# A hybrid decoder layer: the narrow projection groups chained in PSUM, and W_out's plain blocks split early and stored

## The chip, the core and the metric

The kernel runs on one core of one Trainium2 chip. The metric is the device time of one execution in microseconds (us). The engines go by the profile's names: PE multiplies matrices (PEld loads its weights), DVE works elementwise, ACT evaluates functions and copies, POOL is a second, slower elementwise engine, and SP only issues transfers. Transfers can be issued by SP, ACT and POOL; each of these works through its instructions in order, and an issue that waits holds up what is behind it on its queue.

## The reference

One layer over 2048 tokens of width 1024, in float32:

```
n = rmsnorm(x);  proj = n @ w_in          # 3088 columns: gq gk gv gr glow dq dk dv
o_a = gated linear attention(gq, gk, gv, gate from glow), normed, times silu(gr)
o_b = dilated sliding-window attention(dq, dk, dv), three (window, dilation) pairs, with a bias table
h = x + [o_a ; o_b] @ w_out
h = h + square(relu(rmsnorm(h) @ w_ff1)) @ w_ff2
y = rmsnorm(h)
```

## The kernel before

**Exact products from two parts.** Matmuls run in a reduced float type. So each operand is split into a high part (an ACT copy) and a low part (a DVE subtraction), and `mm3` (L139 to L142) adds three matmuls: high by high, low by high, high by low. The helper `split` (L489 to L491) does the two instructions for one tile.

**Products of blocks.** The big products use a seven-multiplication scheme on two-by-two blocks: the two halves of the tokens or of the columns, and the two halves of the inner dimension. Sums of blocks are formed in SBUF ahead, the products are numbered 1 to 7, and the result blocks c11, c12, c21 and c22 are sums of products.

**The stages.** First the projection (`jobs`, L749 to L768, about 20 to 520 us), then attention, with the gated linear attention woven into it (`units`, L1242 to L1266, to about 865 us), then the product with W_out (L1556 to L1610), then the two MLP products.

**The projection.** The tokens are taken in two halves. In each half there are nine groups of W_in's columns (`groups`, L249): `dv`, then `gr` with the gate's 16 columns (264 wide), then six narrow ones (`dq`, `dk`, `dq`, `dk`, `gq`, `gk`, 2 x 128 columns), then `gv`. A narrow group puts the weights on the stationary side and streams 512 tokens, so one of its products is 12 matmuls of 512 columns; a product of a wide group is 4 x 12 matmuls of 256 or 264. A job is one product of one group. Each job first prepares the weights of the job after next (`prep`, L278: an ACT copy and a DVE subtraction into one of three `wcomb` buffers, and sums of weight blocks in the two `wraw` buffers, with the next group's loads behind them, `load_w`, L267), then multiplies (`product`, L400) into a PSUM bank, and then `rest` (L422) reads the bank.

Before, every product has a bank of its own, taken in turn ("acao", L372). ACT copies products 1, 5 and 4 (L440, L445, L453); DVE adds for products 2, 6, 3 and 7 (L442, L447, L448, L450, L455) and makes two more sums (L458). `outputs` (L323) exchanges the buffers of c12 and c22 from group to group. `finish` (L329) stores a result block: for `dq` and `dk` it splits it first (L341, L342), for `gr` it works out a log-sigmoid, an exponential and two products (one on POOL, L355), and for the block with the gate's columns `gate` (L308 to L321) transposes, multiplies once on PE and works out another log-sigmoid. Every load of W_in and every store goes through SP. The last two sums of the last job are put off into the attention stage (`late`, L368, L462, L1188).

In the second half the token blocks of that half are made ready beside the products (`second_half`, `OTHER`), and the rows of the attention bias are worked out (`bias_rows`, L469) and spread in DRAM (`spread_bias`).

**W_out.** The rows of some token tiles are multiplied plainly ("plain blocks" of W_out, called 1, 12, 2 and 3: the two column halves of inner rows 0 to 511 and of inner rows 512 to 1023); the other tiles use the seven products, for which blocks 5, 6, 4 and 7 are sums that POOL makes in attention (`sum_wo`) and `mix_wo` splits. The plain blocks are loaded in the last 28 units of attention, 128 rows every third unit (`load_wo`, L1115, called at L1240), and split there: two times 128x512 for inner rows 0 to 511 (`wb`), 128x1024 for the others (`wo`).

**The first MLP product.** Blocks of W1 (256 columns) are loaded through POOL (`load_w1`, L1381), two transfers of 512 KB each; the first two are asked for at the end of the W_out stage (L1607), and `prep1` (L1389) splits them.

**What orders the work.** From L739 on the program's order is a priority, not a fixed order: the compiler plans the order of each engine's instructions with a model of their durations, and the engines then follow that order strictly. `keep_in_program_order` pins an instruction behind the one that the program gives its engine just before it. All big tiles of SBUF come from 25 slots of one size, handed out when the last reader of the old content is done; PSUM's eight banks have the tags a (2), c (3), d (2) and o (1).

## Time and profile before

| | |
|---|---|
| median of 3 runs | 2244.66 us (2239.35 to 2244.89) |
| the profiled execution | 2242.91 us |
| its span on the core | 2241.1 us |
| mean granted clock of PE | 0.997 |
| busy: PE, DVE, ACT, POOL | 99%, 75%, 56%, 24% |
| moved by DMA | 491.79 MB, mean 219 GB/s |

A matmul's record is longer than its turn: the next starts before its end, so the busy time of PE says where PE stood still, not how fast it went. How fast it went is read from the number of matmuls in a stretch and from the granted clock. A group of instructions has, after its count, its busy time and mean duration in ns, and behind the second bar the idle time of its engine just before it, with what ended it. In the view of waits the three numbers are the total in us, how often, and the longest.

### The profile page before, as it was taken

The numbers are of one execution on the slowest core, as the hardware profiler recorded it, in microseconds if no ns is written. First come the engines' busy times: TensorE is split into PE (matmuls) and PEld (weight loads), VectorE is DVE, ScalarE is ACT, GpSimd is POOL, SyncE is SP. The second block draws the span as 40 slices with busy tenths as digits, with TensorE's granted clock in tenths as the row PEclk, the third lists the DMA queues.
The fourth block names the chain that finished last, engine by engine and source line by source line (L and its number), as shares of the span: only waits on it lengthen the run. The fifth ranks groups of instructions, "written<-read, shape, count | busy, mean of one in ns | idle before, by whom it ended". The sixth has DMA issues, their size and how long they took to land.

```text
span 2241.1 us, 35330 instructions
## 1 busy us (share of the span) xinstructions
PE 2212.8 (99%) x12420; PEld 1918.8 (86%) x12420; DVE 1680.8 (75%) x3173; ACT 1253.5 (56%) x2506; POOL 533.6 (24%) x535
## 2 busy tenths in 40 slices
PE   9999999999999999999999999999999999999998
PEld 8978998799999998887888888888888888888877
DVE  8787868666677677778777788777685697576798
ACT  7675446435787785555655566555555433333446
POOL 1110001016577673000000000000006222031462
PEclk9999999999999999999999999999999999999999
DMA  6467854787977877767744456555489988677775
GB/s 214 141 188 229 256 165 121 213 250 251 312 256 222 271 214 241 247 225 249 220 141 149 140 177 199 165 167 167 130 279 287 306 282 276 216 250 253 250 258 197
DMA packets 340934, 491.79 MB, mean 219 GB/s; under 512 B 20503, under 2 KB 237162, under 8 KB 330004
## 3 DMA queue, kind: packets, MB, share of 16 engines
q1 hardware_dynamic: 319842, 394.88, 54.6%
q0 software_dynamic: 13568, 41.95, 7.6%
q10 hardware_dynamic: 7346, 52.70, 6.3%
q8 instruction: 98, 1.61, 0.3%
q14 instruction: 80, 0.66, 0.1%
HBM read 335.52 MB, written 158.66 MB: 221 GB/s over the span
## 4 chain that ended last, share of the span: by engine, by line
PE 68%; issue 16%; DVE 7%; DMA 5%; POOL 2%; ACT 1%; SPq 0%; POOLq 0%; ACTq 0%; DVEq 0%
PE ps_a L141 7%; PE ps_a L142 6%; PE ps_a L140 6%; PE ps_c L141 5%; PE ps_c L142 5%; PE ps_c L140 5%; PE ps_a L909 4%; PE ps_d L141 3%; PE ps_d L142 3%; PE ps_d L140 3%; PE ps_o L141 3%; PE ps_o L140 3%; PE ps_o L142 3%; PE ps_d L890 3%; PE ps_c L872 2%
## 5 line engine op out<-in xcount | busy, mean ns | idle before, releaser
L490 ACT ACTIVATE cb<-bs 128x1024 fp32r<-128x1024 f32 x104 | 110.1, 1059 | 287.9 <-PE ps_o L141 94.6
L491 DVE TENSOR_TENSOR cb<-bs,cb 128x1024 fp32r<-128x1024 f32 x104 | 157.9, 1519 | 137.7 <-ACT cb L490 137.4
L1680 POOL TENSOR_TENSOR bs<-bs,rb 128x1024 f32<-128x1024 f32 x60 | 174.3, 2912 | 318.1 <-DMA bs<-w_ff 282.4
L491 DVE TENSOR_TENSOR w1comb<-w1raw,w1comb 128x512 fp32r<-128x512 f32 x224 | 153.2, 686 | 94.0 <-ACT w1comb L490 93.9
L1387 POOL DMA_DIRECT2D w1raw<-w_ff x64 | 48.2, 754 | 702.6 <-DVE w1comb L491 532.8
L490 ACT ACTIVATE w1comb<-w1raw 128x512 fp32r<-128x512 f32 x224 | 139.9, 627 | 92.0 <-PE ps_c L142 27.2
L881 ACT ACTIVATE pe<-pe,O 128x256 f32<-128x256 f32 (+1 forms) x384 | 157.5, 454 | 45.6 <-DVE O L880 41.9
L909 PE MATMUL ps_a<-v,pt 128*128 128x65 f32 x1200 | 180.8, 253 | 1.5 <-DVE pt L899 1.4
L909 PEld LDWEIGHTS ps_a<-v,pt 128*128 128x128 f32 x1200 | 175.7, 195 | 2.9 <-DVE pt L899 1.7
L880 DVE CUSTOM_DVE_ANT_0 pe<-ps_c,nb 128x256 f32<-128x256 f32 (+1 forms) x384 | 126.7, 360 | 46.8 <-PE ps_d L890 16.5
L890 PE MATMUL ps_d<-ident,pe 128*128 128x128 f32 x600 | 160.5, 281 | 0.0
L288 ACT ACTIVATE wcomb<-wraw 128x512 fp32r<-128x512 f32 (+2 forms) x119 | 90.1, 757 | 99.2 <-PE ps_a L141 33.0
L140 PE MATMUL ps_c<-hb,w1comb 128*128 128x512 f32 x320 | 124.6, 390 | 0.0
L141 PE MATMUL ps_c<-hb,w1comb 128*128 128x512 f32 x320 | 124.4, 389 | 0.0
L142 PE MATMUL ps_c<-hb,w1comb 128*128 128x512 f32 x320 | 124.1, 389 | 0.0
L491 DVE TENSOR_TENSOR ca<-ra,ca 128x1024 fp32r<-128x1024 f32 x84 | 121.8, 1451 | 0.1
L141 PE MATMUL ps_c<-cb,ca 128*128 128x512 f32 x312 | 121.5, 389 | 0.0
L140 PE MATMUL ps_c<-cb,ca 128*128 128x512 f32 x312 | 121.5, 389 | 0.0
L142 PE MATMUL ps_c<-cb,ca 128*128 128x512 f32 x312 | 121.4, 389 | 0.0
L890 PEld LDWEIGHTS ps_d<-ident,pe 128*128 128x128 f32 x600 | 109.2, 186 | 0.3
L355 POOL TENSOR_TENSOR acc<-acc,misc 128x264 f32<-128x264 f32 (+1 forms) x32 | 29.4, 924 | 319.3 <-DVE acc L354 303.9
L140 PE MATMUL ps_a<-wcomb,tb 128*128 128x256 f32 (+1 forms) x344 | 97.7, 284 | 0.0
(476 smaller groups left out, 7248.8 us busy)
## 6 DMA issues: line engine op xcount, KB each, us to landing
ra<-actD ACTq DMA_DIRECT2D x50, 1024.0 KB, 7.3
actD<-ring SPq DMA_DIRECT2D x176, 256.0 KB, 3.1
rb<-w_ff SPq DMA_DIRECT2D x88, 512.0 KB, 5.3
bs<-w_ff SPq DMA_DIRECT2D x72, 512.0 KB, 6.0
w1raw<-w_ff POOLq DMA_DIRECT2D x64, 512.0 KB, 5.3
k<-kD SPq DMA_DIRECT2D x16, 1024.0 KB, 7.9
rb<-hTD SPq DMA_DIRECT2D x28, 512.0 KB, 5.8
wraw<-w_in SPq DMA_DIRECT2D x48, 256.0 KB, 3.6
```

What stands on the lines that cost most here:

```text
L140: T.matmul(out, sh, mh, start=first, stop=False, **kw)
L141: T.matmul(out, sl, mh, start=False, stop=False, **kw)
L142: T.matmul(out, sh, ml, start=False, stop=last, **kw)
L288: A.activation(hi, src, AF.Copy, scale=sc)
L490: A.activation(hi, src, AF.Copy)
L491: V.tensor_tensor(lo, src, hi.bitcast(F32), op=OP.subtract)
L880: V.tensor_tensor_reduce(p, s, bias, scale=1.0, scalar=BIG, op0=OP.add, op1=OP.min, accum_out=nm)
L881: A.activation(p, p, AF.Exp, bias=nm, scale=-1.0)
L890: T.transpose(pb[:, i * 128:i * 128 + 128], src, ident)
L909: T.matmul(self.b.opsum[:, n % 4], self.pt[:, i * 128:i * 128 + 128], self.b.v[:, blk, cols], start=first, stop=last)
L1387: G.dma_start(raw1[g % 2][:, 4 * k:4 * k + 4], w1[:, 4 * k:4 * k + 4, g0:g0 + 256])
L1680: (engines or ((G,), (V, V))[len(sums) - 1])[e].tensor_tensor(v, v, r, op=OP.add if op == "+" else OP.subtract)
```

## The change

1. **Narrow groups chained.** The order of products is 1, 2, 6, 5, 7, 3, 4 there. Products 6, 7 and 4 are added in PSUM to product 1's bank, and 3 to product 5's; between two links the bank is read. So ACT copies three banks (after 1, 6 and 5), DVE adds three times (2, 7, 3), and c21 is read straight from the bank. The order of the wide groups becomes 1, 2, 5, 6, 3, 7, 4.
2. **Loads.** Two narrow groups share the two `wraw` buffers by halves, so that the next narrow group is asked for while this one is worked on. Wide groups from the third on load through POOL, and `gr`'s stores go through POOL.
3. **Backlog of `gr`.** Its c21 block is finished by one token tile in each of the next four narrow jobs, and the gate's product on PE comes one product later than its transpose. The postponed sums of the last job are gone. `bias_rows` is cut in three steps, and its PSUM tag changes.
4. **W_out.** In the second half's narrow groups two to five, `split_wo` loads W_out through POOL (128 rows, 512 KB, at a time), splits it in 16 pieces of 128x512 (four to a group, two behind the job of product 6 and two behind that of product 5, in two piece buffers), and stores high and low parts through POOL (512 KB a piece). In attention eight transfers of 1 MB, one every third unit, take the place of load and split.
5. **W1.** The second block is loaded as four transfers, the first half of its columns first.

```diff
-    order = (1, 2, 5, 6, 3, 4, 7)
-    jobs = [(g, j) for g in range(2 * NG) for j in order]
+    order, linked = (1, 2, 5, 6, 3, 7, 4), (1, 2, 6, 5, 7, 3, 4)
+    chained = lambda g: groups[g % NG][2] == 128
+    jobs = [(g, j) for g in range(2 * NG) for j in (linked if chained(g) else order)]
+    swapped = [False, False]
+    for g in range(2, 2 * NG):
+        swapped.append(swapped[-1] == chained(g - 1))
...
+    def raw_of(g, n):
+
+        w = groups[g % NG][2]
+        if w > 128:
+            return raws[n][:, :, :, :w]
+        return view(raw_slots[n][:, GP * (g % NG % 2):], (2, 4, 128))
...
-            SP.dma_start(raws[n][:, k, :, :w], w_in[:, 4 * k:4 * k + 4, c0 + n * w:c0 + n * w + w])
+            (SP if g < 2 or chained(g) else G).dma_start(raw_of(g, n)[:, k], w_in[:, 4 * k:4 * k + 4, c0 + n * w:c0 + n * w + w])
...
+        if chained(g):
+            if j == 2:
+                V.tensor_tensor(a11, a21, a11, op=OP.subtract)
+                V.tensor_tensor(a12, a12, a11, op=OP.subtract)
+            if j == 6:
+                V.tensor_tensor(a11, a22, a11, op=OP.subtract)
...
+        for n, k in FREE[g][j]:
+            load_w(g + 1, n, k)
+
+    FREE = {}
+    for g in range(2 * NG):
+        if not chained(g):
+            FREE[g] = {5: [(0, 0)], 3: [(0, 1)], 4: [(1, 1)], 7: [(1, 0)]}
+            if chained(g + 1):
+                FREE[g] = {5: [(0, 0), (0, 1)], 7: [(1, 0), (1, 1)]}
+        elif chained(g + 1):
+            FREE[g] = {1: [(0, 0)], 2: [(0, 1)], 6: [(1, 1)], 5: [(1, 0)]}
+        else:
+            FREE[g] = {1: [(0, 0)], 2: [(1, 0)], 3: [(0, 1)], 4: [(1, 1)]}
...
-            SP.dma_start(srD[tk, j:j + m], s[:, :m])
+            G.dma_start(srD[tk, j:j + m], s[:, :m])
...
-        if e == 0:
-            held[j, i] = bank()
-        p = held[j, i - e]
+        root = {6: 1, 7: 1, 4: 1, 3: 5}.get(j, j) if chained(g) else j
+        if e == 0 and root == j:
+            held[j, i] = ps({1: "a", 2: "c", 5: "oc"[g % 2]}[j]) if chained(g) else bank()
+        p = held[root, i - e]
...
+            if chained(g):
+                if j in (1, 6):
+                    A.activation(ix, q, AF.Copy)
+                elif j == 5:
+                    A.activation(i22, q, AF.Copy)
+                elif j == 4 and kind in ("dq", "dk"):
+                    done((1, 0), q=q)
+                elif j == 4:
+                    A.activation(i21, q, AF.Copy)
+                    done((1, 0))
+                else:
+                    v, y, of = {2: (i11, ix, (0, 0)), 7: (i22, i22, (1, 1)), 3: (i12, ix, (0, 1))}[j]
+                    V.tensor_tensor(v, q, y, op=OP.add)
+                    done(of)
...
+                if kind == "gr":
+                    behind.append((done, (1, 0)))
+                else:
+                    done((1, 0))
...
+    def split_wo():
+
+        raw, pieces = view(slot("wsum"), (2, D)), view(slot("wsplit", FR), (2, 2, 512))
+        for c in range(2):
+            G.dma_start(raw[:, c], wo[:, c])
+        yield
+        for n in range(16):
+            c, h = divmod(n, 2)
+            p = pieces[:, h]
+            r = raw[:, c % 2, 512 * h:512 * h + 512]
+            tc.keep_in_program_order(A.activation(p[:, 0], r, AF.Copy))
+            V.tensor_tensor(p[:, 1], r, p[:, 0].bitcast(F32), op=OP.subtract)
+            G.dma_start(wsD[((1, 12), (2, 3))[c // 4][h]][c % 4 // 2, :, c % 2], p.bitcast(F32))
+            if h and c < 6:
+                G.dma_start(raw[:, c % 2], wo[:, c + 2])
+            yield
...
+        if at == 7 * NG + 9:
+            next(of_wo)
+        if NG + 3 <= g < NG + 7 and jobs[at][1] in (6, 5):
+            for _ in range(2):
+                next(of_wo)
...
-    def load_wo(n):
-        for _ in range(n):
-            c = (4, 0, 1, 5, 2, 3, 6, 7)[len(loaded)]
-            loaded.append(c)
-            raw = slot("woraw")[:, :D]
-            SP.dma_start(raw, wo[:, c])
-            if c < 4:
-                for j, n in ((1, 0), (12, 1)):
-                    split(*block_view(j, c), raw[:, 512 * n:512 * n + 512])
-            else:
-                w = WO[c - 4] = view(slot("wo", FR), (2, D))
-                split(w[:, 0], w[:, 1], raw)
+    def load_wo(j, h):
+
+        t = slot(f"wb{j}", FR, 2048)
+        WB[j, h] = view(t, (2, 2, 512))
+        SP.dma_start(t.bitcast(F32), wsD[j][h].rearrange("p c i n -> p (c i n)"))
...
-        at_unit(NU - 28 + 3 * i + AHEAD, load_wo, 1)
+        at_unit(NU - 28 + 3 * i + AHEAD, load_wo, *((1, 0), (12, 0), (1, 1), (12, 1), (2, 0), (3, 0), (2, 1), (3, 1))[i])
...
-            for k in halves:
-                G.dma_start(raw1[g % 2][:, 4 * k:4 * k + 4], w1[:, 4 * k:4 * k + 4, g0:g0 + 256])
+            for n in range(2) if g == 1 else (None,):
+                cs = slice(0, 256) if n is None else slice(128 * n, 128 * n + 128)
+                for k in halves:
+                    G.dma_start(raw1[g % 2][:, 4 * k:4 * k + 4, cs], w1[:, 4 * k:4 * k + 4, g0:g0 + 256][:, :, cs])
```

124 lines of the change are left out of this document (66 added, 58 removed).

## The prediction

> **What bounds the kernel now.** I read the busy shares first, then matmul counts and the granted clock by stage, then what TensorE waited for, and last the order of time around each wait.
>
> ```profile
> span 2241.1 us, 35330 instructions
> PE 2212.8 (99%) x12420; PEld 1918.8 (86%) x12420; DVE 1680.8 (75%) x3173; ACT 1253.5 (56%) x2506; POOL 533.6 (24%) x535
> ```
>
> TensorE is busy for 99% of the span and idle for 2241.1 - 2212.8 = 28.3 us. The change takes no matmul out, so all it can win is idle time, and time at a low clock. Busy time hides the second, so the stages come next (columns: the stretch and its length, then busy time and count of PE, PEld, DVE, ACT, POOL, then granted clock, DMA share, GB/s).
>
> ```profile
> 1550.00:1600.00 50.00, 50.00 (x223) 41.39 (x222) 38.23 (x83) 27.93 (x48) 4.49 (x6) 1.00 0.53 162
> 380.00:460.00 80.00, 76.84 (x331) 61.67 (x330) 58.01 (x101) 38.16 (x75) 0.72 (x1) 0.98 0.73 214
> 530.00:540.00 10.00, 10.00 (x94) 9.90 (x93) 9.21 (x34) 7.21 (x17) 5.17 (x6) 1.00 0.99 377
> 400.00:410.00 10.00, 9.78 (x37) 7.80 (x38) 8.89 (x17) 6.59 (x15) 0.00 (x0) 0.83 0.42 133
> 820.00:830.00 10.00, 6.89 (x41) 6.25 (x40) 9.34 (x30) 8.60 (x22) 9.85 (x9) 0.69 0.59 187
> 830.00:840.00 10.00, 10.00 (x95) 10.00 (x95) 7.71 (x27) 8.37 (x26) 2.06 (x3) 0.97 0.97 281
> 1040.00:1050.00 10.00, 7.52 (x38) 6.08 (x37) 8.33 (x12) 3.57 (x9) 0.03 (x1) 1.00 0.84 293
> ```
>
> An undisturbed stretch does 223 matmuls of 512 columns in 50 us, 0.224 us each, so a product of a narrow group (12 matmuls) lasts 2.69 us. Two places lose clock: (1 - 0.83) x 10 = 1.7 us at 400, and (0.31 + 0.03) x 10 = 3.4 us at 820 to 840. Next is what PE waited for in the three stages that the diff touches: projection (100 to 520), attention's end (790 to 870), the start of the first MLP product (1000 to 1070).
>
> ```profile
> PE ps_a L140 <- ACT acc L445: 2.0, 1, 2.0
> PE ps_a L141 <- DVE wcomb L292: 0.8, 2, 0.5
> PE ps_o L141 <- DVE wcomb L290: 0.7, 1, 0.7
> PE ps_c L141 <- DVE wcomb L290: 0.6, 1, 0.6
> ```
> ```profile
> PE ps_c L870 <- DVE O L880: 1.6, 1, 1.6
> PE ps_a L909 <- DVE pt L899: 1.4, 1, 1.4
> ```
> ```profile
> PE ps_d L140 <- ACT w1comb L490: 3.0, 2, 2.5
> ```
>
> The three stages wait 4.1, 3.0 and 2.5 us (the longest). With the clock losses, the prize is 4.1 + 1.7 = 5.8, 3.0 + 3.4 = 6.4 and 2.5 us: **14.7 us**.
>
> **The change part by part.**
>
> *Narrow groups chained, loads earlier.* The 2.0 us wait in order of time:
>
> ```profile
> 391.79 0.52 SPq L343 DMA_DIRECT2D qD<-acc  x1
> 399.57 0.60 ACT L445 ACTIVATE acc<-ps_a 128x512 f32<-128x512 f32 x1 [5.65 <-DMA qD<-acc]
> 400.22 0.56 PE L140 MATMUL ps_a<-tb,wcomb 128*128 128x512 f32 x1 [2.02 <-ACT acc L445]
> ```
>
> ACT stood 5.65 us in front of a copy into an accumulator whose store had not landed (7.8 us after its issue), and PE lost 2.02 of them, then the clock. The new order leaves six products between a c22 store and its rewriting by the next narrow group, 6 x 2.69 = 16 us, against five in the old one, and the store no longer sits behind a whole `gr` backlog, which is now handed out one token tile per job. I count this wait and its clock loss as gone, 3.7 us. The three `wcomb` waits (2.1 us) come from a crowded DVE, whose groups between 360 and 480 (six narrow groups) are:
>
> ```profile
> L288 ACT ACTIVATE wcomb<-wraw 128x512 fp32r<-128x512 f32 (+1 forms) x41 | 26.6, 649 | 25.8 <-PE ps_a L142 7.9 <-DVE wraw L294 6.3 <-PE ps_c L142 3.7
> ...
> L342 DVE TENSOR_TENSOR acc<-acc 128x512 f32<-128x512 f32 x16 | 11.2, 702 | 0.1
> L341 ACT ACTIVATE acc<-acc 128x512 fp32r<-128x512 f32 x16 | 9.9, 634 | 10.2 <-DVE acc L458 7.4 <-DVE acc L442 1.6 <-DVE acc L450 0.9
> L458 DVE TENSOR_TENSOR acc<-acc 128x512 f32<-128x512 f32 (+1 forms) x12 | 7.7, 682 | 0.0
> ...
> L442 DVE TENSOR_TENSOR acc<-ps_a,acc 128x512 f32<-128x512 f32 x3 | 2.8, 935 | 0.0
> ```
>
> Chaining cuts a narrow group's seven result additions to three. Gone are one from PSUM (0.94), the two of L458 (2 x 0.68) and L448's (priced as L458, 0.68): 3.0 us; one lo part is now subtracted straight from PSUM, 0.94 for 0.70. Net 2.7 us of DVE less per group. ACT keeps three copies. I take half of the 2.1 us as won, 1.0. **Won here: 4.7.**
>
> New is a chain: products 6, 7, 3 and 4 add to a bank that ACT or DVE must have read first. One other product, 2.69 us, lies between each pair. The copy (0.94 as the nearest PSUM read) with one prep and one hi copy ahead of it (0.65 + 0.63) takes 2.2 us and fits; with two of each it takes 3.5 and PE waits 0.8. Over 12 narrow groups with four links each the cost lies between 0 and 38 us; on the nearest row, DVE lateness seen four times in twelve groups, I take 1.0, just behind the two `gr` groups.
>
> Wide loads and the `gr` stores go to POOL's queue. POOL is busy for 0.72 of the 80 us from 380, and a wide load waits behind no `gr` product, so I take 0, hidden under two jobs of lead; without that cover it is a late group start, about 2 us each time. The moved `bias_rows`, the new order of the wide groups and the two postponed sums cost 0: the PE waits above name no line of theirs, and DVE instructions are moved, not added.
>
> *W_out's plain blocks.* In four narrow groups of the second half, 16 pieces of 128x512 are split: ACT 16 x 0.65 = 10.4 us, DVE 16 x 0.70 = 11.2, against the 4 x 2.7 = 10.8 us that chaining frees on DVE. DVE stays near 58 of 80 us; ACT goes from 38 to 49. PE isn't touched unless an engine stands in line. It can: two piece buffers serve four pieces in two neighbouring jobs, so the third piece waits until the first one's store has landed. With ready work ordered ahead of it that costs PE nothing; in program order it costs 2.3 to 4.8 us in each group (first rival). Choice: 0.5 each, **2.0 lost**, nearer to the free end, since the preparation for the next two jobs is ready before the store can land.
>
> Removed at attention's end are the splits, which take (view of the groups from 795 to 865):
>
> ```profile
> L491 DVE TENSOR_TENSOR wb<-woraw,wb 128x512 fp32r<-128x512 f32 x8 | 8.5, 1076 | 1.3 <-ACT wb L490 1.3
> ...
> L491 DVE TENSOR_TENSOR wo<-woraw,wo 128x1024 fp32r<-128x1024 f32 x4 | 6.2, 1560 | 0.2 <-ACT wo L490 0.2
> ```
>
> In order of time they stand right ahead of both waits (the 3.47 is two subtractions):
>
> ```profile
> 817.88 3.47 DVE L491 TENSOR_TENSOR wb<-woraw,wb 128x512 fp32r<-128x512 f32 x2 [0.93 <-ACT wb L490]
> ...
> 822.09 0.39 PE L870 MATMUL ps_c<-k,qs 128*128 128x256 f32 x1 [1.63 <-DVE O L880]
> ...
> 824.08 1.98 DVE L491 TENSOR_TENSOR wo<-woraw,wo 128x1024 fp32r<-128x1024 f32 x1
> ```
>
> DVE gets 14.7 us back, so both waits go, and with them the low clock behind them; next late is the combination of the last heads, which POOL slows. Of 6.4 us I take **5.4 won**. In the splits' place come eight loads of 1 MB, at the eight places of the loads of 0.5 MB:
>
> ```profile
> w1raw<-w_ff POOLq DMA_DIRECT2D x64, 512.0 KB, 5.3
> k<-kD SPq DMA_DIRECT2D x16, 1024.0 KB, 7.9
> ```
> ```profile
> L1120 SPq DMA_DIRECT2D woraw<-w_out x8: 332/459/1687, 797.4 to 843.9; - x8
> ```
> ```profile
> 869.33 0.50 PE L140 MATMUL ps_a<-wb,mT 128*128 128x512 f32 x1 [0.52 <-DVE O L912]
> ```
>
> At 7.9 us (the `kD` row, of the same size) they land well ahead: the last is issued near 843.9, and the first product with W_out starts at 869.33, 25 us later. They add 4 MB to a stage whose DMA share reaches 0.97. SP passes a load on only when its slot is free, and stores queue behind it; I take 0 (hidden by those 25 us), at worst 3 us at the next stage's start.
>
> *The second W1 block in column halves.*
>
> ```profile
> 1038.54 1.50 POOL L1387 DMA_DIRECT2D w1raw<-w_ff  x2 [11.35 <-PE ps_a L142]
> ...
> 1046.81 0.63 ACT L490 ACTIVATE w1comb<-w1raw 128x512 fp32r<-128x512 f32 x1 [6.37 <-DMA w1raw<-w_ff]
> ```
>
> Two issues of 0.75 become four. The half that is needed first should land near 1038.54 + 0.75 + 5.3 = 1044.6 by the median, 2.2 us sooner than ACT's start at 1046.81; but rows are half as long, so I take **1.5 won**, between 0 and 2.5.
>
> **Sum:** 4.7 + 5.4 + 1.5 - 1.0 - 2.0 = 8.6 us. The profiled execution took 2242.91 us, 1.8 us around its span, so 2234.3. The median of the runs shown, 2244.66, is 1.75 higher and would give 2236.1; I say **2235.0**.
>
> **The rivals.**
>
> *The third piece stands in ACT's line (slower).* Place: four groups between 380 and 460. With product 6 ending at 0, ACT has copied it at 0.94, the first piece's store issues at 0.94 + 0.65 + 0.70 = 2.3 and lands after 5.3 (`w1raw`'s median) to 7.8 us (the store at 391.79), at 7.6 to 10.1; the second follows 0.75 later. ACT then does two pieces, and the next prep adds 0.65 + 0.70: ready at 10.4 to 12.9, where product 4 was due at 3 x 2.69 = 8.1. PE loses 2.3 to 4.8 us, and 1.7 of clock as at 400: 4 to 6.5 a group, 16 to 26 in all in place of the 2.0. That gives 2248 to 2258. It decides from (8.6 + 2.0) / 4 = 2.7 us a group. For it speaks the 5.65 us wait above, which is this very kind; against it that PE lost only 2.02 of those.
>
> *DMA is full.* From 380 to 460, 214 GB/s run; 4 MB read and 8 MB written more are 12.6 MB / 80 us = 157 GB/s, together 371. The fullest stretch quoted moved 377 at a share of 0.99. Then loads and stores come late, projection wins nothing (4.7) and loses some 2 us: 2241.7. Against it: loads are now asked for five products ahead. The Trainium skill, DMA: Bandwidth & Descriptors, Specifications, puts the limit of HBM for one core at about 358 GB/s, which would make 371 too much; the 377 measured here speak against so low a limit.
>
> *The low clock stays.* If it isn't tied to the waits, 1.7 + 3.4 = 5.1 us aren't won: 2235.0 + 5.1 = 2240.1. For it: the wait of 2.48 us at 1045 cost no clock (1.00). Against it: both low stretches lie right behind the longest waits of their stages. The Trainium skill, TensorE: Matmul & The Clock Gate, Part 1, has the clock halved after an idle window of about 3.4 us; by that rule waits of 1.4 to 2.0 us would halve nothing. The two rows at 400 and 820 lean the other way.
>
> **How the numbers follow.** What a measurement of this kernel can tell from no change is about 0.3%, 6.7 us: faster is below 2237.9, slower above 2251.4. Forecast 0.54 (own range 2228 to 2239: 0.50 faster, 0.04 same); pieces in line 0.24 (0.22 slower, 0.02 same); DMA full 0.12 (0.08 same, 0.04 slower); clock stays 0.10 (0.02 faster, 0.08 same). Faster 0.52, same 0.22, slower 0.26. The range goes from 2226 (2242.91 - 14.7 = 2228, and the runs' scatter) to 2254, inside the slower rival.
>
> **What would show it.** Right: no PE wait on L880 or L899 near 820 and a clock of 1.00 there; no ACT wait on a `qD` store near 400; a shorter wait on `w1comb`. Wrong: ACT waits on a store of the split pieces with PE idle and the clock under 1 between 380 and 460, PE waits on reads of chained banks behind `gr`, or a DMA share near 1 there with late `wraw`. New waits at places the diff doesn't name, since the order of the engines is planned anew, would also undo it.

## The result and the profile after

The kernel after takes 2247.19 us (median of 18 runs, 2241.65 to 2255.19) against 2239.89 us (median of 18 runs of the kernel before on the same chip, 2237.34 to 2245.01). The ratio is 1.0028, 95% interval 1.0019 to 1.0038: about 7 us **slower**, where 8.6 us faster was forecast. The loss is small: 2247.19 lies inside the stated range of 2226 to 2254 and 0.28% is just under the 0.3% that the prediction took as tellable, though the interval leaves no room for a gain. It also comes within 1 us of the first rival's 2248 to 2258, but not by that rival's mechanism, so that nearness is luck. The profiled execution took 2250.91 us.

The page after, its span and its busy times:

```profile
span 2249.1 us, 35367 instructions
...
PE 2213.7 (98%) x12420; PEld 1919.4 (85%) x12420; DVE 1644.1 (73%) x3129; ACT 1251.2 (56%) x2500; POOL 572.7 (25%) x609
```

DVE does 37 us less, as planned, and PE's 12420 matmuls are the same. PE's idle time went from 28.3 to 2249.1 - 2213.7 = 35.4 us. So an engine with a load of 75% was relieved (to 73%), and PE waited longer. Where, the stages tell (us; the projection up to its last matmul, then from one stage's last matmul to the next one's; one profiled execution each):

| | projection | attention | W_out | first MLP product | second |
|---|---|---|---|---|---|
| before | 520.3 | 342.7 | 192.3 | 613.3 | 564.2 |
| after | 525.3 | 338.1 | 198.5 | 614.1 | 564.8 |
| difference | +5.0 | -4.6 | +6.2 | +0.8 | +0.6 |

Attention's end won nearly what was forecast (5.4). The projection lost where 1.7 were forecast as won (4.7 - 1.0 - 2.0), and the W_out stage lost 6.2 where 1.5 were forecast as won (the wait of 2.5 us on `w1comb` at 1045 lies ahead of its last matmul). Of the 6.2, 2.0 us are a matter of the border: the planned order puts 34 matmuls of the first MLP product ahead of W_out's last one where before has 25, and 9 x 0.224 = 2.0 us so change stage. With the first MLP product, which has no such shift at its end, the two take 812.6 us in place of 805.6: 7.0 more. The windows after that answer to those quoted before (columns as there):

```profile
400.00:410.00 10.00, 6.99 (x19) 5.39 (x20) 8.36 (x15) 6.76 (x14) 1.23 (x3) 0.66 0.96 357
...
820.00:830.00 10.00, 10.00 (x91) 9.74 (x90) 7.69 (x27) 7.47 (x22) 10.00 (x9) 1.00 0.88 298
830.00:840.00 10.00, 10.00 (x95) 9.90 (x95) 6.59 (x28) 9.02 (x30) 3.81 (x6) 1.00 1.10 370
...
920.00:930.00 10.00, 9.96 (x45) 8.09 (x45) 9.34 (x15) 3.86 (x7) 0.00 (x0) 0.83 0.57 180
```

At 820 the two waits are gone and the clock is 1.00, as forecast. At 400 both are worse: 19 matmuls in 10 us instead of 37, at 0.66 instead of 0.83. And at 920 stands a low clock that before doesn't have. What PE waited for in the same three stages, after (total us, times, longest; first the projection from 100, then attention's end from 790, then the W_out stage up to 1070):

```profile
PE ps_d L345 <- DVE acc L208: 4.9, 1, 4.9
PE ps_d L353 <- DVE acc L208: 2.4, 2, 1.8
PE ps_a L140 <- ACT acc L484: 0.7, 1, 0.7
```
```profile
PE ps_c L1440 <- DMA mx<-mixD: 1.5, 1, 1.5
```
```profile
PE ps_a L140 <- ACT w1comb L545: 2.3, 2, 1.5
PE ps_d L140 <- ACT mcomb L545: 2.2, 1, 2.2
PE ps_d L140 <- ACT w1comb L545: 2.1, 1, 2.1
```

In the projection none of the waits of before is left; the two longest that replace them are waits of the **gate** (L345 its transpose, L353 its product) for DVE's part of the log-sigmoid (L208). The long one in order of time:

```profile
391.99 1.52 SPq L541 DMA_DIRECT2D rbD<-rowD  x2
...
393.23 0.57 POOL L397 DMA_DIRECT2D srD<-acc  x1 [0.30 <-POOL acc L396]
...
400.55 1.03 ACT L382 ACTIVATE acc<-ps_a 128x512 fp32r<-128x512 f32 x1 [6.87 <-DMA srD<-acc]
401.61 1.02 DVE L383 TENSOR_TENSOR acc<-ps_a,acc 128x512 f32<-128x512 f32 x1 [6.72 <-ACT acc L382]
402.53 0.42 DVE L208 SCALAR_TENSOR_TENSOR acc<-ps_d,acc 128x256 f32<-128x256 f32 x1
...
403.01 0.41 PE L345 MATMUL ps_d<-ident,small 128*50 128x128 f32 x1 [4.92 <-DVE acc L208]
```

A postponed tile of `gr` is stored from its c21 buffer at 393.23; ACT has to rewrite that buffer for the next narrow group and stands in front of the store for 6.87 us; DVE's subtraction needs ACT's copy and stands 6.72 us; the gate's instruction on DVE is queued behind it, and PE's transpose waits for that. Before, one narrow product waited 2.02 us at the same place. So the old wait on a store was traded for one of the same kind on another buffer, with a longer chain behind it. Two parts of the change bring the store to this moment together: the run without the postponed block (no_behind, below) has its last `srD` store at 381.84, and the one with the gate uncut (chain_gate, which also leaves out the W_out part) at 382.65; neither has a PE wait at 400 to 420.

The first half shows what chaining itself does. Windows of before, then of after:

```profile
110.00:120.00 10.00, 10.00 (x47) 8.17 (x46) 9.93 (x21) 9.09 (x23) 3.54 (x4) 1.00 0.28 81
120.00:130.00 10.00, 10.00 (x47) 7.98 (x46) 8.98 (x19) 8.35 (x23) 2.62 (x4) 1.00 0.60 188
...
150.00:200.00 50.00, 48.99 (x226) 39.69 (x225) 43.97 (x71) 29.67 (x60) 0.00 (x0) 1.00 0.75 235
```
```profile
110.00:120.00 10.00, 7.45 (x26) 5.58 (x25) 9.37 (x21) 6.45 (x17) 5.36 (x8) 0.77 0.50 161
120.00:130.00 10.00, 10.00 (x42) 8.03 (x42) 3.47 (x7) 6.41 (x16) 0.00 (x0) 0.88 0.45 139
...
150.00:200.00 50.00, 50.00 (x239) 41.56 (x238) 42.06 (x65) 30.48 (x57) 0.00 (x0) 1.00 0.83 257
```

Counts mislead where matmuls differ in size: of the 13 more between 150 and 200, eight are the transposes of 128 columns. In columns streamed it is 7 x 512 more, so 7 x 0.224 = 1.6 us won. Between 110 and 130, right behind `gr`, it is 24.75 x 512 fewer, 5.5 us lost: there stand the gate's second wait (1.83 us) and a clock of 0.77 and 0.88.

The same count tells where the projection falls behind. At the moment when before has streamed a given number of columns, after is behind by 6.2 us at 129 (behind the first `gr`), by 2.2 at 188, 2.0 at 328, 8.7 at 396 (behind the second `gr`), 5.6 at 414, and 4.9 from 441 to the end. So the chained groups of the first half win back 4 us, waits of before included, and the loss arises behind the two `gr` groups.

### The profile page after: what moved, and what is told of

Read it like the earlier page. It is cut to its first block, busy times and chain, and to the rows that moved or that the text cites. A ratio compares the mean times of both kernels' runs of the same rounds, so it can differ in the third digit from the quotient of the medians.

```text
span 2249.1 us, 35367 instructions
## 1 busy us (share of the span) xinstructions
PE 2213.7 (98%) x12420; PEld 1919.4 (85%) x12420; DVE 1644.1 (73%) x3129; ACT 1251.2 (56%) x2500; POOL 572.7 (25%) x609
## 4 chain that ended last, share of the span: by engine, by line
PE 68%; issue 15%; DMA 7%; DVE 6%; ACT 2%; POOL 2%; SPq 0%; POOLq 0%; DVEq 0%; ACTq 0%
PE ps_a L141 7%; PE ps_a L142 7%; PE ps_a L140 7%; PE ps_c L141 5%; PE ps_c L140 5%; PE ps_c L142 5%; PE ps_a L997 4%; PE ps_d L141 3%; PE ps_d L140 3%; PE ps_d L142 3%; PE ps_d L978 3%; PE ps_o L140 3%; PE ps_o L142 3%; PE ps_o L141 3%; PE ps_c L960 2%
## 5 line engine op out<-in xcount | busy, mean ns | idle before, releaser
L305 DVE TENSOR_TENSOR wcomb<-wraw,wcomb 128x512 fp32r<-128x512 f32 (+2 forms) x77 | 74.5, 967 | 35.7 <-ACT wcomb L303 35.5
```

The lines of the kernel that those rows point to most:

```text
L305: V.tensor_tensor(lo, src, hi.bitcast(F32), op=OP.subtract)
```

## Experiments

Theories at the start: **(a)** the projection's loss comes with the postponed `gr` block and the gate cut in two, not with W_out; **(b)** it is the split pieces, in ACT's line (the first rival on record) or as traffic (the second); **(c)** what makes single stores land so late is the spreading of the bias beside them (L541). For the W_out stage: the eight loads of 1 MB, or the W1 halves. Each kernel was timed in several rounds against the kernel before on its chip. All figures of stages are from one profiled execution each, so a difference under about 2.5 us in one of them carries nothing: w1_whole, which differs from after only behind 1030, has an attention 2.4 us longer. In the kernels with the W_out part at attention's far end, the 2.0 us of the moved border are in the W_out column; before, traffic_only, split_only and bias_late don't have them, no_wout and chain_gate have 1.1.

| kernel | projection | attention | W_out | ratio to before | 95% interval |
|---|---|---|---|---|---|
| no_wout | 524.6 | 345.2 | 189.9 | 1.0026 | 1.0013 to 1.0040 |
| only_wout | 527.1 | 339.5 | 196.4 | 1.0041 | 1.0027 to 1.0055 |
| no_behind | 526.0 | 337.8 | 194.1 | 1.0036 | 1.0020 to 1.0053 |
| later | 524.5 | 338.8 | 195.3 | 1.0039 | 1.0026 to 1.0053 |
| bias_gr | 528.0 | 340.8 | 201.2 | 1.0049 | 1.0033 to 1.0065 |
| no_behind_four | 522.8 | 337.6 | 195.9 | 1.0015 | 1.0005 to 1.0025 |
| chain_gate | 522.3 | 343.2 | 192.5 | 1.0011 | 0.9999 to 1.0023 |
| w1_whole | 526.0 | 340.5 | 197.9 | 1.0024 | 1.0011 to 1.0036 |
| only_wout_four | 531.0 | 337.4 | 197.8 | 1.0043 | 1.0028 to 1.0058 |
| wout_early | 530.8 | 350.8 | 200.6 | 1.0104 | 1.0083 to 1.0125 |
| combo | 532.5 | 340.8 | 195.6 | 1.0042 | 1.0027 to 1.0058 |
| bias_late | 516.9 | 351.3 | 191.9 | 1.0020 | 1.0004 to 1.0037 |
| traffic_only | 527.6 | 343.1 | 191.0 | 1.0033 | 1.0021 to 1.0045 |
| split_only | 527.2 | 341.4 | 191.8 | 1.0037 | 1.0023 to 1.0051 |
| loads_only | 520.8 | 337.1 | 195.8 | 1.0021 | 1.0010 to 1.0032 |

**The two halves of the change.** no_wout is the kernel after with W_out's loads and splits as before; only_wout is the kernel before with the W_out part alone (`split_wo`, and in attention the line below).

```diff
-        at_unit(NU - 28 + 3 * i + AHEAD, load_wo, 1)
+        at_unit(NU - 28 + 3 * i + AHEAD, load_wo, *((1, 0), (12, 0), (1, 1), (12, 1), (2, 0), (3, 0), (2, 1), (3, 1))[i])
```

> The changed kernel with its W_out part undone: plain blocks loaded and split at attention's end as before. Stages by the last PE matmul of each, before and changed: projection to 520.3 and 525.3 us, attention 342.7 and 338.2 long, W_out stage 192.3 and 198.5. Theory A (the postponed gr block makes the projection's loss by itself: its store is late and ACT stands in front of the buffer): the projection still ends near 524 to 526, with a PE wait of 2 us or more on the gate's chain behind gr in the second half. Theory B (the 12 MB of the split make it, by slowing that store): the wait near 400 falls under 1 us and the projection ends at 519 to 522. Either way attention is back at 342 to 344. If the W_out stage's loss comes from the W_out part, that stage is back at 192 to 194; if it is from the new W1 loads or only from the newly planned order, it stays at 196 or more. Time: A 2243 to 2250, B 2236 to 2242.

> The kernel before with the W_out part alone: pieces split behind products 5 and 6 of the second half's narrow groups two to five, stored through POOL, loaded in eight transfers at attention's end. Theory A: no postponed gr block, so no PE wait of over 3 us in the projection; it ends at 519 to 523, attention is 337 to 339 long. Theory B: the traffic of the split delays the qD store near 392 further, PE waits 4 us or more near 400 and the projection ends at 524 or later. W_out stage: 198 if the loss there belongs to the W_out part, 192 to 194 if not. Time: A with the stage unharmed 2234 to 2238, A with the stage's loss 2240 to 2244, B 2244 or more.

Either half alone makes the kernel slower. no_wout has no split traffic and no piece, and PE's longest wait in its projection is the same one:

```profile
PE ps_d L345 <- DVE acc L208: 5.1, 1, 5.1
```

So (a) holds for that wait. only_wout has neither a postponed block nor a cut gate, and loses 6.8 us in the projection: (b) holds too. The places differ: by columns, only_wout is 2.2 us behind at 414 and 6.4 at 441, and no_wout 3.5 at 368 and 8.7 at 396. Its longest PE wait is 2.4 us, at 432, and not the 4 us near 400 that was expected under (b). The losses don't add up (4.3 and 6.8 alone, 5.0 together); that an engine which stands in one line lets the other's work pass is a guess, which no run shows. What does separate is what comes behind attention: W_out and the first MLP product take 805.8 us without the W_out part, as before (805.6), and 811.1 with it alone.

**The postponed block and the piece buffers.** no_behind finishes `gr`'s c21 at once; no_behind_four also has four piece buffers instead of two; later shifts the split by one group.

```diff
-                if kind == "gr":
-                    behind.append((done, (1, 0)))
-                else:
-                    done((1, 0))
+                done((1, 0))
...
-        raw, pieces = view(slot("wsum"), (2, D)), view(slot("wsplit", FR), (2, 2, 512))
+        raw = view(slot("wsum"), (2, D))
+        pieces = [view(slot("wsplit", FR), (2, 2, 512)) for _ in range(2)]
...
-            p = pieces[:, h]
+            p = pieces[c % 2][:, h]
```
```diff
-        if NG + 3 <= g < NG + 7 and jobs[at][1] in (6, 5):
+        if NG + 4 <= g < NG + 8 and jobs[at][1] in (6, 5):
```

> The changed kernel, but the c21 block of gr is finished at once with product 4 and not put off by one token tile a job into the next narrow group. Theory A: ACT's wait of 6.87 us on the srD store and the PE wait of 4.92 us near 400 go, so does the 1.83 us wait at 115; projection ends at 517 to 521, time 2238 to 2242. Theory B (traffic, not the postponing): PE still waits 3 us or more near 400 and the projection ends at 523 or later.

> The run without the postponed gr block, with four piece buffers for the split of W_out in place of two. If the third piece standing in ACT's line makes what is left of the projection's loss there (ACT waits 9.3 us on stores of pieces, PE 2.43 us near 430): ACT's wait on wsD falls under 1 us, the PE wait near 430 goes, and the projection ends at 520 to 523 in place of 526. If it is the traffic itself, PE still waits 1.5 us or more between 400 and 450 and the projection ends at 525 or later. The W_out stage stays as it is, 193 to 196.

> The changed kernel with the split of W_out one narrow group later (groups three to six of the second half instead of two to five), away from gr's postponed stores. Theory A: the postponed block is as late as before the shift, so a PE wait of 2 us or more stays near 400; but the one at 115 in the first half, where nothing is split, stays in any case. Theory B: near 400 the wait falls under 1 us, projection ends at 519 to 521. Time: A 2244 to 2250, B 2240 to 2243.

In no_behind the wait at 400 is gone, and the first rival's wait stands in its place: ACT in front of a piece buffer whose store hasn't landed (first fence), and PE behind DVE's low part (second).

```profile
ACT wsplit L813 <- DMA wsD<-wsplit: 9.3, 2, 5.1
```
```profile
PE ps_a L141 <- DVE wcomb L305: 2.4, 1, 2.4
```

With four buffers no such wait of ACT is left, and the projection ends 3.2 us earlier (522.8), which leaves 2.5 of the loss. The ratio is lower too (1.0015 against 1.0036), but the intervals overlap, so that the kernel gains isn't shown. later keeps the postponed block and still has the gate's wait (2.6 us at L345) and two of 2.0 and 1.4 on `wcomb`: a shift by one group only moves the collision.

**Why single stores land so late.** In both kernels two spreads of the bias are issued at 392 (L486 before, L541 after), beside the store that is waited for. bias_gr issues all the spreads of the kernel after earlier, in the `gr` group; bias_late issues those of the kernel before 19 jobs later.

```diff
-        if 7 * NG + 8 <= at < 7 * NG + 44 and at % 3 == 0:
-            spread_bias(2 - (at - 7 * NG - 8) // 12, (at - 7 * NG - 8) // 3 % 4 * 2)
+        if 7 * NG + 7 <= at < 7 * NG + 13:
+            for n in range(2 * (at - 7 * NG - 7), 2 * (at - 7 * NG - 7) + 2):
+                spread_bias(2 - n // 4, n % 4 * 2)
```

> The changed kernel with the twelve transfers that spread the bias rows issued in the second half's gr group (about 305 to 350 us), two a job, and none left near 392. Theory A (the postponed gr block is at fault by its position): the srD store's landing stays at 7 us and PE still waits 4 us or more near 400. Theory C (the two rbD spreads issued at 392 hold the store up, as they held the qD store in the kernel before, and the postponed block only puts another waiter behind them): the longest landing of an srD store falls from 7.2 us to under 4, the PE wait near 400 under 1.5 us, and the projection ends 4 to 8 us earlier, at 517 to 522. Time: A 2246 to 2250, C 2239 to 2243.

> The kernel before, with the twelve spreads of bias rows issued 19 jobs later (jobs 90 to 123 in place of 72 to 105), so that none is near 392, and nothing else changed. If two spreads at 392 make the qD store land after 7.8 us and ACT wait 5.65 us: ACT's wait falls under 2 us, the PE wait of 2.02 us near 400 and the low clock behind it go, the projection ends at 516 to 518, and the time is 2 to 5 us under the kernel before. If not (the store is late because of the whole gr backlog), the wait stays at 1.5 us or more and the time is within 2 us of it.

ACT's wait between 380 and 420 on the same store, in bias_gr:

```profile
ACT acc L382 <- DMA srD<-acc: 0.3, 1, 0.3
```

Of 6.9 us 0.3 are left, with the postponed block in place; in bias_late the wait on the `qD` store falls from 5.65 to 2.5 us, no PE wait is left at 400, and the projection ends 3.4 us earlier than before. So (c) is shown for the long landing: 7.2 us from the issue at 393.23 to the copy at 400.55, beside two spreads; in bias_gr no `srD` store takes more than 2.6 us. The projection of bias_gr ends at 528.0 all the same, where 517 to 522 was expected, and bias_late's wait stays over the 2 us that was expected. But the spreads cost at their new places too. In bias_gr PE waits 3.3 us at 354 for an addition on DVE, and the kernel is slower still; in bias_late attention's first unit waits (PE from 380 to 560):

```profile
PE ps_c L870 <- POOL qp L823: 4.1, 1, 4.1
```

**The gate.** chain_gate is no_wout with the gate's product issued right behind its transpose, as before the change; combo is no_behind_four with the same edit.

```diff
-        gated.append(t)
-
-    def gate_product(t):
-
-        gT = gTs[t % 2]
...
-            ready = gated[:]
             product(at, i)()
-            for t in ready:
-                gate_product(t)
-                gated.remove(t)
```

> The changed kernel with the W_out part undone and the gate's product back in one piece with its transpose. If cutting the gate in two makes the first half's waits (1.8 and 0.8 us at 114, with a low clock behind them): they go, and the first half is 3 to 5 us shorter; if the chained banks or the postponed gr block make them, a PE wait of 1.5 us or more stays between 105 and 125. The wait of 5 us near 400 is not expected to change by more than 2 us under either.

> The changed kernel with the three mends that the runs point to: gr's c21 finished at once, the gate in one piece, four piece buffers. If the projection's loss is these three and nothing else, it ends at 517 to 521 (before 520.3, changed 525.3), with no PE wait of over 1.5 us in it; if each mend only uncovers the next wait in line, one of 1.5 us or more stays and it ends at 521 to 525. The W_out stage stays at 194 to 198, so the time is 2238 to 2242 or 2242 to 2247.

chain_gate has the lowest ratio (1.0011), which can't be told from before, nor from no_wout's 1.0026, whose interval overlaps. The wait of 5 us at 400 is gone, though it was expected to stay: uncut, the gate lets the last postponed store leave at 382.65 and not at 393, ahead of the two spreads, and it lands within 3.3 us. So in these traces the wait takes both the postponed block and the cut gate. The first half does not get the 3 to 5 us that were expected of a cut gate's price: by columns chain_gate is 4.5 us behind at 129 and 2.5 at 328, against 5.9 and 1.6 in no_wout. Other waits stand there, 2.9 us on reads of chained banks among them (PE from 100 to 535):

```profile
PE ps_a L140 <- ACT acc L479: 2.9, 3, 1.8
```

In combo the same edit helps nothing: its projection ends at 532.5, with a PE wait of 4.9 us on `wcomb` behind late `wraw`, which no_behind_four doesn't have. A mend that is good beside one half of the change isn't beside the other.

**What of the W_out part costs in the projection.** only_wout_four is only_wout with four piece buffers. traffic_only adds to the kernel before only the loads and as many stores of unsplit data, split_only only the loads and the 32 instructions; both keep the W_out stage of before.

```diff
+            p = view(raw[c % 4 // 2][:, c % 2], (2, 512))
+            G.dma_start(wsD[((1, 12), (2, 3))[c // 4][h]][c % 4 // 2, :, c % 2], p)
```
```diff
+            tc.keep_in_program_order(A.activation(p[:, 0], r, AF.Copy))
+            V.tensor_tensor(p[:, 1], r, p[:, 0].bitcast(F32), op=OP.subtract)
```

> The kernel before with the W_out part alone, and four piece buffers in place of two. With two buffers it took 527.1 us to the projection's end, 339.5 in attention and 196.4 in the W_out stage (before: 520.3, 342.7, 192.3). If pieces in ACT's line are the whole cost of the split there: ACT waits on wsD for under 1 us, the waits of 1.6 and 2.4 us at 410 and 430 go, the projection ends at 519 to 522. If the added traffic also counts: one of the two waits stays, 523 to 527. The W_out stage keeps its 195 to 198 in either case, attention 338 to 340. Time 2238 to 2243 or 2243 to 2248.

> The kernel before, and in the four narrow groups of the second half only the traffic that the W_out part adds there: 8 loads of 0.5 MB of W_out's plain blocks through POOL's queue and 16 stores of 0.5 MB of what was loaded, unsplit. No piece is split there, no engine but POOL's queue is used, and the W_out stage splits the blocks as before. Theory that the 12 MB themselves delay the loads of wraw: the projection ends 4 to 9 us later than the 520.3 us of before, with PE waits of over 1.5 us near 400 to 440 behind splits of late wraw, and the rest of the kernel is as before: ratio 1.002 to 1.004. Theory that it is the pieces in ACT's and DVE's line: the projection ends within 1.5 us of before, ratio within 0.9990 to 1.0010.

> The kernel before, with the 8 loads of W_out's plain blocks and the 16 splits of pieces in ACT's and DVE's line in the four narrow groups of the second half, but no store of the pieces; nothing reads them, and the W_out stage loads and splits the blocks as before. Theory that the instructions cost by themselves: projection 2 to 5 us later than 520.3, ratio 1.001 to 1.002. Theory that only the stores (the wait of a piece for its buffer, and 8 MB of traffic) cost: projection within 1.5 us of before, ratio within 0.9990 to 1.0010.

With four buffers only_wout doesn't get faster: the longest PE wait moves from 2.4 to 4.8 us, at 428, in this window:

```profile
420.00:440.00 20.00, 14.85 (x53) 11.41 (x52) 13.52 (x21) 7.42 (x13) 1.60 (x3) 0.83 1.04 390
```

and DVE waits for the weights to be loaded (DVE between 380 and 460):

```profile
DVE wraw L294 <- DMA wraw<-w_in: 4.7, 1, 4.7
```

That is the second rival: 390 GB/s at a share of 1.04, against 215 in the same window of before. That the transfers run ahead once no piece holds the stores back is argued and not shown: only_wout has the same share, 1.04, in this window, at 353 GB/s. (The Trainium skill, DMA: Bandwidth & Descriptors, Specifications, puts the limit of HBM for one core at about 358 GB/s; 390 over 20 us speak against it here.)

traffic_only has no piece in any engine's line and loses 7.2 us. Its transfers wait for no splits, so they run earlier than in the change, mostly between 330 and 380 (246 GB/s, where before moves 114), and hit the `gr` stores there: one issue on SP's queue stands for 7.41 us and one for 4.33 (second fence, timeline), and PE waits (third fence, 300 to 535). In before the longest in that stretch took 3.1 us each (first fence):

```profile
336.35 6.24 SPq L271 DMA_DIRECT2D wraw<-w_in  x2
```
```profile
328.78 7.41 SPq L356 DMA_DIRECT2D srD<-acc  x1
...
337.88 4.33 SPq L486 DMA_DIRECT2D rbD<-rowD  x1
```
```profile
PE ps_a L140 <- DVE acc L447: 3.9, 1, 3.9
PE ps_a L140 <- ACT acc L445: 3.3, 1, 3.3
```

split_only has no stores and loses 6.9 us, by smaller waits and a granted clock of 0.84 from 400 to 420 and of 0.91 from 440 to 460 (PE's waits, 300 to 535):

```profile
PE ps_a L141 <- DVE wcomb L292: 2.4, 2, 1.9
PE ps_a L140 <- ACT acc L445: 2.3, 1, 2.3
```

Neither the stores nor the instructions is the only cause: with the loads, each costs some 7 us, and both together cost 6.8 (only_wout). Both runs contain the eight loads through POOL, which no run has alone in the projection, so the loads may be what the two share. Since traffic_only's transfers don't lie where the change has them either, how the 6.8 us of only_wout divide stays open.

**The W_out stage.** w1_whole is the kernel after with whole W1 blocks. wout_early is only_wout_four with the eight loads 12 units earlier. loads_only is the kernel before with only the eight loads of 1 MB, in place of loads and splits; it splits and stores nothing in the projection, and loads what another stage has stored (`nTD`).

```diff
-            for n in range(2) if g == 1 else (None,):
+            for n in (None,):
```
```diff
-        at_unit(NU - 28 + 3 * i + AHEAD, load_wo, *((1, 0), (12, 0), (1, 1), (12, 1), (2, 0), (3, 0), (2, 1), (3, 1))[i])
+        at_unit(NU - 40 + 3 * i + AHEAD, load_wo, *((1, 0), (12, 0), (1, 1), (12, 1), (2, 0), (3, 0), (2, 1), (3, 1))[i])
```
```diff
+        SP.dma_start(t.bitcast(F32), nTD[(1, 12, 2, 3).index(j)].rearrange("p c n -> p (c n)"))
```

> The changed kernel with the second W1 block in two transfers of 512 KB again. If column halves do any good, the wait on w1comb near 1046 grows from 2.1 us to 3 or more; if four transfers only make each land later (8.6 us against 5.3), it shrinks to 1.5 or less. Since no instruction of other engines changes, all stages before 1030 stay within 1 us of the changed kernel's but for the clock. Time within 2 us of the changed kernel either way.

> As only_wout_four, with the eight loads of the split parts 12 units (about 25 us) earlier in attention. If these loads hold up the loads of mixD at the start of the W_out stage (PE waits 1.9 us on mx near 853, and mx takes 8.5 us in place of 5.5 to land): the wait near 853 goes, mx lands in 5 to 6 us, and the W_out stage falls to 192 to 194. If the stage's loss is only the newly planned order of ACT and SP there (W1's and wtD's blocks in line): the stage stays at 195 or more, whatever becomes of the wait near 853.

> The kernel before with the W_out part at its far end alone: W_out's plain blocks come as eight loads of 1 MB at the places of the loads of 0.5 MB, with no split near attention's end. Nothing is split or stored in the projection: the loads take 1 MB each of what another stage stored, so the product is one with other numbers in place of W_out's plain blocks. Theory that the eight loads of 1 MB make the W_out stage late: projection as before (520.3, within 1.5), attention 2 to 4 us shorter than 342.7, the W_out stage 196 to 199 instead of 192.3, ratio within 0.9995 to 1.0015. Theory that the W_out stage's 4 to 6 us come with what the split did to the order of the engines or to memory: the W_out stage stays at 190 to 193, attention is 3 us shorter, ratio 0.997 to 0.999.

loads_only has the projection of before, and shows the gain and the loss of this part by itself. Attention is 5.6 us shorter, with one wait left from 790 to 870, and the clock at 1.00 where before had 0.69:

```profile
PE ps_c L1356 <- DMA mx<-mixD: 1.1, 1, 1.1
```
```profile
820.00:830.00 10.00, 10.00 (x99) 10.00 (x98) 6.88 (x27) 8.78 (x27) 7.42 (x9) 1.00 0.98 352
```

Then the W_out stage and the first MLP product take 811.0 us instead of 805.6: in this execution 5.4 us are given back. That `mx`, the first operand of the W_out stage, is awaited here, and not before, points at loads. SP's issues around attention's end, of before and then of after (whose waits there are those of loads_only):

```profile
844.57 2.97 SPq L1353 DMA_DIRECT2D mx<-mixD  x4
...
850.83 1.11 SPq L1353 DMA_DIRECT2D mx<-mixD  x2
...
853.56 0.38 SPq L1147 DMA_DIRECT2D wtraw<-wtD  x1
...
859.07 0.52 SPq L984 DMA_DIRECT2D mixD<-gla  x1
```
```profile
843.88 1.90 SPq L1214 DMA_DIRECT2D wb<-wsD  x2
845.87 2.14 SPq L1423 DMA_DIRECT2D mx<-mixD  x4
...
856.83 0.52 SPq L1072 DMA_DIRECT2D mixD<-gla  x1
...
857.45 1.19 SPq L1423 DMA_DIRECT2D mx<-mixD  x2
...
859.72 1.14 SPq L1220 DMA_DIRECT2D wtraw<-wtD  x2
```

The first four loads of `mx` are issued right behind the last two of the 1 MB loads, and the DMA is full a little later (after, 850 to 855):

```profile
850.00:855.00 5.00, 3.46 (x35) 3.18 (x33) 3.06 (x10) 3.13 (x13) 3.63 (x6) 1.00 1.02 401
```

But before moves 406 GB/s at the same share from 855 to 860. Attention ends at 863.0 and 863.4, and the next loads of `mx` and `wtraw` leave 6.6 and 6.2 us later than before: 5.9 us ahead of attention's end where it was 12.2. In loads_only it is the same (5.6). What stands directly in front of them is a store, not a load: in the new order SP issues the store of `mixD` at 856.83 ahead of them, and in before the store of that kind is behind them, at 859.07. For it SP stands 5.3 us, as ACT is late (SP's waits from 840 to 870, after):

```profile
SPq L1072 <- ACT gla L1174: 5.3, 1, 5.3
```

It isn't shown that these late loads cost more than the wait of 1.1 to 1.5 us on `mx`. Counted in columns from attention's end, loads_only is level with before until 1033, 170 us later; it falls behind at the change to the first MLP product, by 1.4 us at 1055, 4.0 at 1085 and 4.5 at 1113. After falls 4.5 us behind earlier, by 923: there stand the wait of 2.2 us on `mcomb` and the clock of 0.83. So the 1 MB loads, with the order of the engines that was planned anew around them, cost 5.4 us (loads_only) to 7.0 (after) behind attention, at places that differ; how, stays open.

The profiled execution of loads_only, 2242.09 us, lies 3.5 us below the median of its 11 runs (2245.55); the other runs lose more than these stages show, and where, no trace tells. Its ratio, 1.0021, is above what was expected under either theory. In wout_early the loads of `mx` are early again (the last leaves 7.7 us ahead of attention's end) and PE waits on none of them, yet the stage takes 200.6 us, and W_out with the first MLP product 815. By what was expected before it ran, that speaks against the late loads and for the planned order; but attention is disturbed too, so it doesn't settle it. Earlier loads are no mend: in wout_early attention takes 350.8 us, and PE's waits from 790 to 870 are on the gated linear attention (`gla`, up to 2.3 us), whose loads stand behind the W_out loads on SP.

W1's halves win nothing: with whole blocks the stage takes 197.9 instead of 198.5 us, and the three waits on `w1comb` come to 3.9 instead of 4.4. Their rows say why (1030 to 1070: w1_whole, then after):

```profile
w1raw<-w_ff POOLq DMA_DIRECT2D x4, 512.0 KB, 7.4
```
```profile
w1raw<-w_ff POOLq DMA_DIRECT2D x2, 512.0 KB, 7.9
w1raw<-w_ff POOLq DMA_DIRECT2D x4, 256.0 KB, 8.6
```

Half the bytes in rows of half the length, four issued together, landed later than whole blocks.

## Why the prediction was wrong, step by step

Three steps failed: the wait at 400 that the term "won here: 4.7" counts as gone, the eight loads that were priced at nothing, and the 1.5 us of W1. The 2.0 us for the split were too little where it stands alone.

- *"I count this wait and its clock loss as gone, 3.7 us."* **Failed.** The c22 wait did go (after has none on a `qD` store). But that `gr`'s backlog "is now handed out one token tile per job" was counted only as a gain. A tile handed out late is a store from c21 in the midst of narrow groups that rewrite c21, the very kind of wait quoted for before. It cost 4.92 us and a clock of 0.66 in place of 2.02 us and 0.83: 18 matmuls, 4.0 us. The step looked only at which buffer was awaited before, and not at the next buffer whose store the same two spreads would hold up (bias_gr: 6.9 to 0.3 us).
- *The gate cut in two* was not priced at all. It is half of that wait: with the postponed block and an uncut gate (chain_gate) the last store leaves 10.6 us sooner and the wait at 400 is gone. What the cut costs by itself behind the first `gr` group is not shown: after waits 1.83 us there, at a low clock, but chain_gate is behind there too, by 4.5 us at 129.
- *Chain, 1.0 lost; wcomb waits, 1.0 won.* Right in size in the change: the waits on chained banks come to 0.7 us there, the `wcomb` waits of after are gone (before had four, in three rows, and not three), and 150 to 200 wins 1.6 us. In chain_gate the waits on chained banks come to 2.9.
- *Split, 2.0 lost.* In size too small where it stands alone: 6.8 us (only_wout). Both rivals named mechanisms that the runs show: the third piece (no_behind: 5.1 us of ACT) and the full DMA (only_wout_four: 390 GB/s and `wraw` 4.7 us late). In the change itself it hardly shows: the projection of no_wout ends 0.7 us sooner, within the scatter. Why, no run shows.
- *Attention's end, 5.4 won.* Right: 4.6 in the change, 5.6 in loads_only, by the waits and the clock that were named.
- *Eight loads of 1 MB, "I take 0 (hidden by those 25 us), at worst 3".* **Failed.** The 25 us were a misreading: 869.33 is only the first matmul of that line which waited, and before multiplies with W_out's plain blocks from 858.54 on, so the lead was 14.6 us.

```profile
858.54 0.48 PE L140 MATMUL ps_d<-wb,mT 128*128 128x512 f32 x1
```

The loads are in time even so: in after the last leaves at 845.4 and lands within 7.2 us, and is first needed at 859.2. Yet W_out and the first MLP product take 5.4 us more in loads_only and 7.0 in the change (with a wait of 2.2 us on `mcomb` and a low clock at 920). The sum asked only whether the moved transfers land in time. That SP's order is planned anew around them, and that loads of the next stage leave 6 us later by it, is seen; by which step the 5.4 to 7.0 us come about stays open.
- *W1's halves, 1.5 won.* **Failed**: nothing, by w1_whole; the longest wait on `w1comb` fell from 2.5 to 2.1 us, their sum rose from 3.0 to 4.4. The prediction took the landing of a half as the median of a whole block under lighter load (5.3); under this load it was 8.6.
- *The low clock stays* (third rival) was wrong at 820 and right at 400 in effect: the clock fell behind some waits, in after behind those at 113, 403 and 916, and not behind others: 3.3 us at 354 in bias_gr and 2.5 us at 1045 in before were followed by 1.00. What decides it, these traces don't tell. (The Trainium skill, TensorE: Matmul & The Clock Gate, Part 1, has the clock halved after a free-running idle window of about 3.4 us; 1.63 and 1.40 us at 820 before, and 2.2 us at 916 after, cost it all the same.)

The signs on record read: low stretch at 820 gone, as for right; the DMA share of 1.06 at 420 and new waits at places that the diff doesn't name (`mcomb`), as for wrong. The PE waits behind `gr` are the gate's; those on chained banks, the sign that was named, come to only 0.7 us.

## What to carry to other kernels

When a wait on a buffer's store is to go, list the next buffers of the same ring and ask which stores hold them, and what else is on the DMA at that minute; a wait that a neighbour's transfer causes moves to another buffer and does not vanish. Where the order of the engines is planned anew, an edit can open waits 170 us behind it, so compare kernels by equal work done (columns streamed) and not by stage borders, which move too. In a kernel whose main engine is busy for 99% of the span, an edit that relieves an engine with a load of 75% can win only the waits it has by name, and any new thing in an in-order line can cost as much as it wins.

## What the runs showed of the hardware

- A store of 124 KB lands 7.2 us after its issue beside two transfers of 384 KB that spread a small source, where the median for such stores in that stage is 3.4 us or less and the longest 2.6 us in bias_gr, which issues the spreads earlier.
- Four transfers of 256 KB landed later (8.6 us) than four of 512 KB in the same place (7.4 us).
- One core moved 390 GB/s over 20 us (only_wout_four), and the records put the DMA share there at 1.04.
- An issue can itself take long while the DMA is busy: 7.41 us for one on SP's queue beside POOL's transfers (traffic_only), against 0.52 for the `qD` store at 391.79 in before.
